# Differential attention's queries and keys projected with a head's columns as rows, the rotary step by rows with a row-swapped load, in place of transposes

## The chip, the cores and the metric

The kernel runs on one core of one Trainium2 chip. The core has TensorE (PE, matrix products; its weight loads are shown as PEld), VectorE (DVE), ScalarE (ACT), GpSimd (POOL), SyncE (SP) and 16 DMA engines. The metric is the device time of one launch in microseconds (us): the median of several runs. Beside it there is one execution recorded by the hardware profiler, from which all durations below come.

## The reference, cut to what matters

Two layers of a hybrid backbone work on 640 tokens of 1024 channels: 128 context tokens, and 512 latent tokens, which also read 128 cached context tokens. Each layer projects the normalised tokens and runs three mixers (retention, differential attention, latent attention), merges them by gates, and ends in a SwiGLU block. The change concerns differential attention with 4 heads, each with two halves of 64 columns for queries and keys:

```python
dq = dq.reshape(B, S, H_DIFF, 2, DIFF_HD)          # h @ w_in, columns of 4 heads x 2 x 64
dk = dk.reshape(B, S, H_DIFF, 2, DIFF_HD)
if rope is not None:                               # latent tokens alone
    dq, dk = _rope(dq, c64, s64), _rope(dk, c64, s64)
dk_all = jnp.concatenate([ck.reshape(B, L, H_DIFF, 2, DIFF_HD), dk], axis=1)

def _rope(x, c, s):                                # c, s of a token's row and column
    x1, x2 = jnp.split(x, 2, axis=-1)              # 32 and 32 columns
    return jnp.concatenate([x1 * c - x2 * s, x2 * c + x1 * s], axis=-1)

def _diff_attention(q, k, v, lam, lam_init):
    s = jnp.einsum('bqhcd,bkhcd->bhcqk', q, k) * DIFF_HD ** -0.5
    p = jax.nn.softmax(s, axis=-1)
    a = p[:, :, 0] - lam * p[:, :, 1]
    o = jnp.einsum('bhqk,bkhe->bqhe', a, v)
    return _head_rmsnorm(o) * (1.0 - lam_init)
```

The context tokens' keys and values are outputs too (`ndk`, `ndv`).

## The kernel before, in words

All numbers are 32-bit. A matrix product is made of three products of operands split in two (`mm3`, lines 131 to 133: high x high, high x low, low x high). `split_hi` (ACT, line 112) rounds a tile to the matmul's format, and `split_lo` (DVE, line 115) takes the rest. `load_w` loads one weight tile of 128 x 1024 on SyncE's queue and splits it.

The stages of a layer follow one another: latent attention (`mla`), its branch projection (`branch_first`), differential attention (`diff`), retention (`ret`), the gates and branches, the output projection and the FFN. Into a stage that waits for softmax, units of projection work are put as filler. `plan(points, (generator, n, t0, t1))` spreads n units over a stage's points; `fill()` at each point issues the units that are due, `flush()` the rest. A planner of the framework then orders the instructions of each engine's queue by a simulated time line; every queue is in order.

`diff_proj` is the filler of latent attention: 30 units on 37 points. For each of two pairs of heads (`hp`) and each of keys, queries and values (`kind` 1, 0, 2) it loads two weight tiles, and for each of five blocks of 128 tokens makes 24 matmuls (8 row blocks of the weights by 3 products) of 256 columns: the tokens are the output's rows (`a_gemm`, activations as the loaded operand, weights streaming). ACT copies a result from the PSUM tile `G` into `stg` (line 791), and GpSimd's queue stores it to DRAM in `dproj` (line 792).

`diff` builds each head's operands in `build(hd)`, which stands one head ahead of `diff_head`. It loads values `V`, keys `rk` (`dproj` and the cache `cdk`, 6 blocks of 128 tokens as rows) and queries `rq` on GpSimd's queue. `rope_in_place` (lines 431 to 442, DVE) rotates four blocks in four instructions. For each two blocks of keys ACT makes the high part `kh`, written twice (line 742), and DVE the low part `kl`; TensorE transposes four high tiles (line 747) and two low tiles (line 748) against `identr` into the PSUM tiles `Tp`; ACT clears the first into `K1` (line 750) and DVE the second into `K2z` (lines 751 and 752). Queries go the same way: `qs` (line 762), two transposes for each block (line 767), and the copy into `Q` (line 769). `K1` holds a half's high part twice, over 128 rows; `Q` holds a half's high and low part one above the other; `K2z` holds a half's low part over zeros. With these, two matmuls make the three products (`diff_head`, lines 825 and 826). Tiles `ra` (`rk`, `rq`), `V`, `K1`, `Q` and `K2z` have two buffers each.

In `diff`, 16 units of gates (line 1013) and 20 of retention's values (lines 805 to 809, stored by GpSimd's queue into `rproj`) are the filler, on 23 points, of which `diff` has 20. `ret` loads `rproj` again.

Of the kernel before, what the change touches and what calls it, by code (L numbers as in the profile page):

```python
# [12 lines left out]
F32 = mybir.dt.float32  # L13
# [34 lines left out]
class Kern:  # L48
# [107 lines left out]
    def setup(self):  # L156
# [7 lines left out]
        self.identr = self.const.tile([P, 128], F32R, name="identr")  # L164
        self.dve.tensor_copy(self.identr, self.ident)
# [264 lines left out]

    def rope_in_place(self, pool, x, b, nb, nh, hd, tag):

        cc, ss = (C_C64, C_S64) if hd == 64 else (C_C32, C_S32)
        hh = hd // 2
        c = self.ct[:, cc + hd * b:cc + hd * (b + nb)].rearrange("p (a d) -> p a d", a=nb).unsqueeze(2).to_broadcast([P, nb, nh, hd])
        s = self.ct[:, ss + hd * b:ss + hd * (b + nb)].rearrange("p (a d) -> p a d", a=nb).unsqueeze(2)
        u = pool.tile([P, nb * nh * hd], F32, tag=tag, name="rp", bufs=1).rearrange("p (a h d) -> p a h d", a=nb, h=nh)
        d = self.dve
        d.tensor_tensor(u[:, :, :, 0:hh], x[:, :, :, hh:hd], s[:, :, :, 0:hh].to_broadcast([P, nb, nh, hh]), op=ALU.mult)
        d.tensor_tensor(u[:, :, :, hh:hd], x[:, :, :, 0:hh], s[:, :, :, hh:hd].to_broadcast([P, nb, nh, hh]), op=ALU.mult)  # L440
        d.tensor_tensor(x, x, c, op=ALU.mult)
        d.tensor_tensor(x, x, u, op=ALU.add)
# [252 lines left out]
    def diff(self, l, act, yhi, ylo, ctx):  # L695
# [20 lines left out]
        a6 = "p (a c r) -> p a c r"  # L716

        def build(hd):
            hp, h = divmod(hd, 2)
            hs = slice(128 * h, 128 * h + 128)  # L720
            V[hd] = pool.tile([P, 6, 128], F32, tag="V", name="V", bufs=2)
# [5 lines left out]

            k1 = K1[hd] = pool.tile([P, 2, TK], F32R, tag="K1", name="K1", bufs=2)
            k2 = K2[hd] = k2z[hd % 2]
            r = pool.tile([P, 6, 128], F32, tag="ra", name="rk", bufs=2)  # L730
            nc.gpsimd.dma_start(out=r[:, 0, :], in_=self.dproj[hp, 1][:, 0, hs])
            nc.gpsimd.dma_start(out=r[:, 1, :], in_=io["cdk"][l, :, 128 * hd:128 * hd + 128])
            nc.gpsimd.dma_start(out=r[:, 2:6, :], in_=self.dproj[hp, 1][:, 1:5, hs])
            nc.gpsimd.dma_start(out=io["ndk"][l, :, 128 * hd:128 * hd + 128], in_=r[:, 0, :])
            rv = r.rearrange("p a (c d) -> p a c d", c=2)
            self.rope_in_place(pool, rv[:, 2:6], 0, 4, 2, 64, "rp")
            for j in range(3):
                x = rv[:, 2 * j:2 * j + 2]
                kh = pool.tile([P, 2, 2, 2, 64], F32R, tag="kh", name="kh", bufs=2)
                kl = pool.tile([P, 2, 2, 64], F32R, tag="kl", name="kl", bufs=2)  # L740
                for i in range(2):
                    a.copy(kh[:, i], x[:, i].unsqueeze(2).to_broadcast([P, 2, 2, 64]))
                self.split_lo(kl, x, kh[:, :, :, 0, :])
                t, t2 = self.Tp(F32R), self.Tp(F32R)
                for i in range(2):
                    for c in range(2):
                        self.pe.transpose(t[:, 256 * c + 128 * i:256 * c + 128 * i + 128], kh[:, i, c].rearrange("p a r -> p (a r)"), self.identr)
                    self.pe.transpose(t2[:, 128 * i:128 * i + 128], kl[:, i].rearrange("p a r -> p (a r)"), self.identr)
                cs = slice(256 * j, 256 * j + 256)
                a.copy(k1[:, :, cs], t.rearrange("p (c n) -> p c n", c=2))  # L750
                d.tensor_copy(k2[0:64, 0, cs], t2[0:64, 0:256])
                d.tensor_copy(k2[64:128, 1, cs], t2[64:128, 0:256])

            q = Q[hd] = pool.tile([P, 2, T], F32R, tag="Q", name="Q", bufs=2)
            r = pool.tile([P, 6, 128], F32, tag="ra", name="rq", bufs=2)
            nc.gpsimd.dma_start(out=r[:, 0:5, :], in_=self.dproj[hp, 0][:, :, hs])
            rv = r.rearrange("p a (c d) -> p a c d", c=2)
            self.rope_in_place(pool, rv[:, 1:5], 0, 4, 2, 64, "rp")
            for b0, nb in ((0, 1), (1, 2), (3, 2)):
                x = rv[:, b0:b0 + nb]  # L760
                qs = pool.tile([P, 2, 4, 64], F32R, tag="kh", name="qs", bufs=2)
                a.copy(qs[:, 0:nb, 0:4:3, :], x)
                self.split_lo(qs[:, 0:nb, 1:3, :], x, qs[:, 0:nb, 0:4:3, :])
                t = self.Tp(F32R)
                for i in range(nb):
                    for c in range(2):
                        self.pe.transpose(t[:, 256 * c + 128 * i:256 * c + 128 * i + 128],
                                          qs[:, i, 2 * c:2 * c + 2, :].rearrange("p a r -> p (a r)"), self.identr)
                a.copy(q[:, :, 128 * b0:128 * (b0 + nb)], t.rearrange("p (c n) -> p c n", c=2)[:, :, 0:128 * nb])
# [643 lines left out]
```

## Time and profile before

| | |
|---|---|
| median of 3 runs | 2487.21 us (2484.67 to 2488.88) |
| profiled execution | 2487.65 us, of which the span from first to last instruction 2485.8 |
| PE, PEld | 2419.1 and 2367.1 us busy, 17236 instructions each |
| DVE, ACT, POOL | 1511.3, 992.8 and 177.0 us busy |
| HBM read, written | 225.97 and 20.22 MB, 99 GB/s over the span |

A row of the profile names the line, engine and operation, then what it writes and reads by the program's names (`Tp<-identr,kh`). A busy time is the union of an engine's instructions; matmuls overlap, so that the spacing of their starts, not their duration, is what each takes of the engine. Where a row has a bracket, the engine was idle that long before it, and the arrow names what ended the wait.

### The profile page before, as it was taken

The numbers are of one execution on the slowest core, as the hardware profiler recorded it, in microseconds if no ns is written. First come the engines' busy times: TensorE is split into PE (matmuls) and PEld (weight loads), VectorE is DVE, ScalarE is ACT, GpSimd is POOL, SyncE is SP. The second block draws the span as 40 slices with busy tenths as digits, with TensorE's granted clock in tenths as the row PEclk, the third lists the DMA queues.
The fourth block names the chain that finished last, engine by engine and source line by source line (L and its number), as shares of the span: only waits on it lengthen the run. The fifth ranks groups of instructions, "written<-read, shape, count | busy, mean of one in ns | idle before, by whom it ended". The sixth has DMA issues, their size and how long they took to land.

```text
span 2485.8 us, 42801 instructions
## 1 busy us (share of the span) xinstructions
PE 2419.1 (97%) x17236; PEld 2367.1 (95%) x17236; DVE 1511.3 (61%) x3463; ACT 992.8 (40%) x2102; POOL 177.0 (7%) x306
## 2 busy tenths in 40 slices
PE   8999999999999999999999999998999999999998
PEld 5999999999999999999999999998999999999997
DVE  5877686566787676485477867764663553333324
ACT  5656565422335221212375655653222352122123
POOL 0000210100010010010000012111000000000001
PEclk9999999999999999999999999999999999999999
DMA  6212322322553454463231123213232222222221
GB/s 263 75 60 63 105 78 65 96 91 70 196 175 111 153 178 153 128 193 102 66 126 55 60 75 114 69 61 126 62 109 69 77 68 85 78 69 76 69 75 62
DMA packets 70677, 248.94 MB, mean 100 GB/s; under 512 B 9840, under 2 KB 10064, under 8 KB 69584
## 3 DMA queue, kind: packets, MB, share of 16 engines
q1 hardware_dynamic: 46944, 164.12, 20.3%
q0 software_dynamic: 23248, 81.36, 10.1%
q8 instruction: 135, 2.21, 0.4%
q10 hardware_dynamic: 288, 0.73, 0.1%
q14 instruction: 62, 0.51, 0.1%
HBM read 225.97 MB, written 20.22 MB: 99 GB/s over the span
## 4 chain that ended last, share of the span: by engine, by line
PE 91%; DVE 4%; issue 2%; ACT 2%; DMA 1%; POOL 0%; DVEq 0%; ACTq 0%; POOLq 0%
PE G L131 13%; PE G L132 12%; PE G L133 12%; PE S L1107 8%; PE S L1106 8%; PE S L1105 8%; PE S L131 6%; PE S L132 6%; PE S L133 6%; PE O L855 1%; PE Tp L658 1%; PE S L825 1%; PE O L633 1%; PE O L632 1%; PE S L826 1%
## 5 line engine op out<-in xcount | busy, mean ns | idle before, releaser
L112 ACT CAST whi<-raw 128x1024 fp32r<-128x1024 f32 (+4 forms) x298 | 299.2, 1018 | 756.5 <-PE G L132 262.5
L115 DVE TENSOR_TENSOR wlo<-raw,whi 128x1024 fp32r<-128x1024 f32 (+4 forms) x298 | 349.2, 1182 | 370.7 <-ACT whi L112 368.6
L131 PE MATMUL G<-ghi,whi 128*128 128x256 f32 (+1 forms) x704 | 217.1, 309 | 3.1 <-DVE x L1067 3.1
L133 PE MATMUL G<-ghi,wlo 128*128 128x384 f32 (+1 forms) x704 | 216.4, 308 | 0.0
L132 PE MATMUL G<-glo,whi 128*128 128x384 f32 (+1 forms) x704 | 216.3, 308 | 0.0
L1105 PE MATMUL S<-h1hi,whi 128*128 128x384 f32 x640 | 214.0, 334 | 0.0
L1106 PE MATMUL S<-h1lo,whi 128*128 128x384 f32 x640 | 213.9, 334 | 0.0
L1107 PE MATMUL S<-h1hi,wlo 128*128 128x384 f32 x640 | 213.9, 334 | 0.0
L1107 PE MATMUL S<-h0hi,wlo 128*128 128x256 f32 x704 | 199.2, 283 | 1.1 <-DVE wlo L115 0.9
L1106 PE MATMUL S<-h0lo,whi 128*128 128x256 f32 x704 | 198.8, 283 | 0.0
L1105 PE MATMUL S<-h0hi,whi 128*128 128x256 f32 x704 | 198.1, 282 | 0.0
L238 DVE SCALAR_TENSOR_TENSOR junk<-rawr,csr 128x1024 bf16<-128x1024 f32 x160 | 195.0, 1219 | 1.3
L131 PE MATMUL G<-whi,h1hi 128*128 128x256 f32 x624 | 179.0, 287 | 1.5 <-DVE mx L449 0.6
L133 PE MATMUL G<-whi,h1lo 128*128 128x256 f32 x624 | 177.2, 284 | 0.0
L132 PE MATMUL G<-wlo,h1hi 128*128 128x256 f32 x624 | 177.2, 284 | 0.0
L1067 DVE SCALAR_TENSOR_TENSOR x<-G,mod,x 128x128 f32<-128x128 f32 (+1 forms) x192 | 77.4, 435 | 138.0 <-PE G L133 137.5
L448 DVE TENSOR_REDUCE mx<-S 128x1 f32<-128x640 f32 (+1 forms) x160 | 113.0, 714 | 49.4 <-PE S L826 28.5
L1107 PEld LDWEIGHTS S<-h0hi,wlo 128*128 128x128 f32 x704 | 134.6, 191 | 2.8 <-DVE wlo L115 2.6
L131 PEld LDWEIGHTS G<-ghi,whi 128*128 128x128 f32 x704 | 132.1, 188 | 4.6 <-DVE x L1067 3.4
L1106 PEld LDWEIGHTS S<-h0lo,whi 128*128 128x128 f32 x704 | 134.3, 191 | 0.3
L1105 PEld LDWEIGHTS S<-h0hi,whi 128*128 128x128 f32 x704 | 134.3, 191 | 0.0
L131 PE MATMUL G<-whi,h0hi 128*128 128x256 f32 x416 | 121.6, 293 | 12.0 <-DVE rvs L808 11.7
(431 smaller groups left out, 6901.8 us busy)
## 6 DMA issues: line engine op xcount, KB each, us to landing
raw<-w_ffn_in SPq DMA_DIRECT2D x88, 512.0 KB, 3.6
rawr<-w_adat POOLq DMA_DIRECT2D x80, 512.0 KB, 4.0
raw<-w_gate SPq DMA_DIRECT2D x48, 512.0 KB, 3.3
raw<-w_ffn_out SPq DMA_DIRECT2D x32, 512.0 KB, 3.7
raw<-w_diff SPq DMA_DIRECT2D x24, 512.0 KB, 3.5
raw<-w_branch SPq DMA_DIRECT2D x24, 512.0 KB, 3.6
raw<-w_ret SPq DMA_DIRECT2D x24, 512.0 KB, 3.5
raw<-w_ada SPq DMA_DIRECT2D x16, 512.0 KB, 9.7
```

Source lines behind the costliest of these rows:

```text
L112: (eng or self.act).copy(hi, src)
L115: (eng or self.dve).tensor_tensor(lo, src, hi.bitcast(F32), op=ALU.subtract)
L131: self.pe.matmul(out, lh, rh, start=i == 0, stop=False)
L132: self.pe.matmul(out, lh, rl, start=False, stop=False)
L133: self.pe.matmul(out, ll, rh, start=False, stop=i == n - 1)
L238: self.tc.keep_in_program_order(d.scalar_tensor_tensor(junk, raw, 1.0, self.csr[:, i, :], op0=ALU.mult, op1=ALU.mult, accum_out=mod[:, n, ...
L448: self.dve.tensor_reduce(mx, sv, axis=AX.XY if len(sv.shape) == 3 else AX.X, op=ALU.max)
L632: self.pe.matmul(o[:, :n], vv, hi, start=i == 0, stop=False)
L1067: self.dve.scalar_tensor_tensor(x[h][:, n, c0:c1], ps[:, c0:c1], g[:, n, gi:gi + 1], x[h][:, n, c0:c1], op0=ALU.mult, op1=ALU.add)
L1105: self.pe.matmul(o, lh, rh, start=k == 0, stop=False)
L1106: self.pe.matmul(o, lh, rl, start=False, stop=False)
L1107: self.pe.matmul(o, ll, rh, start=False, stop=k == nk - 1)
```

## The change

Keys and queries are projected head by head with the weights as the loaded operand and the tokens streaming, so that `dproj` for them is a tile of 128 rows (a head's columns) by 640 tokens: 16 units over halves of 256 and 384 tokens, and 10 units of values in the old form, 26 in the plan. `build` loads a head's rows, and for the rotary step a second copy `u` in which blocks of 32 rows are swapped in pairs, by four loads; three DVE instructions then rotate 512 tokens with tables of cosine and sine by rows, loaded once a stage. ACT and DVE write `K1`, `K2z` and `Q` straight from the rows. The key cache comes in and the new keys go out with columns as rows (the host turns them round). The value loads stand behind those of keys and queries.

```diff
-        self.identr = self.const.tile([P, 128], F32R, name="identr")
-        self.dve.tensor_copy(self.identr, self.ident)
...
+        cosT = self.load_small(pool, [P, 512], io["ropeT"][0], "cosT")
+        sinT = self.load_small(pool, [P, 512], io["ropeT"][1], "sinT")
+        def rotate(src, x):
+            u = pool.tile([P, 512], F32, tag="rs", name="rs", bufs=2)
+            for q in range(4):
+                nc.gpsimd.dma_start(out=u[32 * q:32 * q + 32, :], in_=src[32 * (q ^ 1):32 * (q ^ 1) + 32, 128:640])
+            d.tensor_tensor(x, x, cosT, op=ALU.mult)
+            d.tensor_tensor(u, u, sinT, op=ALU.mult)
+            d.tensor_tensor(x, x, u, op=ALU.add)
         def build(hd):
+            top, low = slice(0, 64), slice(64, 128)
+            src = self.dproj[hd, 1]
+            r = pool.tile([P, TK], F32, tag="ra", name="rk", bufs=2)
+            nc.gpsimd.dma_start(out=r[:, 0:128], in_=src[:, 0:128])
+            nc.gpsimd.dma_start(out=r[:, 128:256], in_=io["cdkT"][l, hd])
+            nc.gpsimd.dma_start(out=r[:, 256:TK], in_=src[:, 128:T])
+            nc.gpsimd.dma_start(out=io["ndk"][l, hd], in_=r[:, 0:128])
+            rotate(src, r[:, 256:TK])
+            for c, own, other in ((0, top, low), (1, low, top)):
+                a.copy(k1[own, c, :], r[own, :])
+                a.copy(k1[other, c, :], r[own, :])
+                self.split_lo(k2[own, c, :], r[own, :], k1[own, c, :])
+            src = self.dproj[hd, 0]
+            r = pool.tile([P, TK], F32, tag="ra", name="rq", bufs=2)
+            nc.gpsimd.dma_start(out=r[:, 0:T], in_=src)
+            rotate(src, r[:, 128:T])
+            for c, own, other in ((0, top, low), (1, low, top)):
+                a.copy(q[own, c, :], r[own, 0:T])
+                self.split_lo(q[other, c, :], r[own, 0:T], q[own, c, :])
             V[hd] = pool.tile([P, 6, 128], F32, tag="V", name="V", bufs=2)
...
-            self.rope_in_place(pool, rv[:, 2:6], 0, 4, 2, 64, "rp")
-            for j in range(3):
...
-            self.rope_in_place(pool, rv[:, 1:5], 0, 4, 2, 64, "rp")
-            for b0, nb in ((0, 1), (1, 2), (3, 2)):
...
     def diff_proj(self, l, act, pool):
...
-            for kind in (1, 0, 2):
-                units = self.load_a(self.io["w_diff"][l, hp, kind], 2, 4, 256)
...
+            for hd in (2 * hp, 2 * hp + 1):
+                for kind in (1, 0):
+                    u = self.load_w(self.io["w_dqk"][l, kind, hd], 1024)
+                    for h in (0, 1):
+                        o, w = HALF[h]
+                        ps = self.G()
+                        self.mm3(ps[:, :w], self.b_steps(*u, 0, KT, act, h))
+                        r = pool.tile([P, 384], F32, tag="stg", name="stg", bufs=2)
+                        self.act.copy(r[:, :w], ps[:, :w])
+                        self.pool.dma_start(out=self.dproj[hd, kind][:, o:o + w], in_=r[:, :w])
+                        yield 1
+            units = self.load_a(self.io["w_dv"][l, hp], 2, 4, 256)
...
-                self.plan(37, (self.diff_proj(l, act, pool), 30, 0.0, 1.0))
+                self.plan(37, (self.diff_proj(l, act, pool), 26, 0.0, 1.0))
```

## Rows read from the trace of the kernel before

**Rows 1.** The page: span, busy time by engine with its share and instructions.

```profile
span 2485.8 us, 42801 instructions
PE 2419.1 (97%) x17236; PEld 2367.1 (95%) x17236; DVE 1511.3 (61%) x3463; ACT 992.8 (40%) x2102; POOL 177.0 (7%) x306
```

**Rows 2.** Busy time by stretch: start:end, length, engines, PE's clock, DMA, GB/s.

```profile
85.00:281.00 196.00, 191.94 (x1498) 186.91 (x1498) 147.34 (x347) 117.63 (x274) 20.42 (x37) 1.00 0.21 68
306.00:493.00 187.00, 180.08 (x1386) 175.57 (x1385) 131.00 (x376) 108.34 (x291) 26.35 (x44) 1.00 0.24 77
...
1529.00:1714.00 185.00, 178.01 (x1369) 173.48 (x1368) 128.32 (x370) 107.20 (x287) 24.72 (x41) 1.00 0.24 77
```

**Rows 3.** PE in order of time (start, duration, what), old projection, 99.8 to 101.9 us.

```profile
99.80 0.28 PE L131 MATMUL G<-whi,h1hi 128*128 128x256 f32 x1
...
101.83 0.28 PE L133 MATMUL G<-whi,h1lo 128*128 128x256 f32 x1
```

**Rows 4.** PE in order of time, a gate unit, 329.6 to 331.8 us.

```profile
329.67 0.33 PE L131 MATMUL G<-h1hi,whi 128*128 128x384 f32 x1
...
331.75 0.33 PE L131 MATMUL G<-h1hi,whi 128*128 128x384 f32 x1
```

**Rows 5.** The transposing lines: instructions, duration ns min/median/max, first and last start.

```profile
L747 PE MATMUL Tp<-identr,kh x96: 222/246/306, 298.4 to 1636.3; 128*128 128x128 f32 x96
...
L748 PE MATMUL Tp<-identr,kl x48: 223/228/281, 302.3 to 1637.1; 128*128 128x128 f32 x48
...
L767 PE MATMUL Tp<-identr,qs x80: 222/244/283, 312.7 to 1642.4; 128*128 128x128 f32 x80
```

**Rows 6.** PE in order of time, a run of six transposes, 305.9 to 306.8 us.

```profile
305.90 0.28 PE L133 MATMUL G<-yhi,wlo 128*128 128x256 f32 x1
306.01 0.46 PE L747 MATMUL Tp<-identr,kh 128*128 128x128 f32 x4
306.31 0.33 PE L748 MATMUL Tp<-identr,kl 128*128 128x128 f32 x2
306.47 0.41 PE L131 MATMUL G<-yhi,whi 128*128 128x384 f32 x1
306.72 0.34 PE L132 MATMUL G<-ylo,whi 128*128 128x384 f32 x1
```

**Rows 7.** PE in order of time, a run of two, 331.9 to 332.5 us.

```profile
331.92 0.34 PE L132 MATMUL G<-h1lo,whi 128*128 128x384 f32 x1
332.10 0.29 PE L767 MATMUL Tp<-identr,qs 128*128 128x128 f32 x2
332.22 0.41 PE L133 MATMUL G<-h1hi,wlo 128*128 128x384 f32 x1
332.47 0.34 PE L131 MATMUL G<-h1hi,whi 128*128 128x384 f32 x1
```

**Rows 8.** PE in order of time, the longest waits ahead of transposes, layer 0.

```profile
327.90 0.36 PE L748 MATMUL Tp<-identr,kl 128*128 128x128 f32 x2 [0.37 <-ACT K L750]
...
362.21 0.34 PE L748 MATMUL Tp<-identr,kl 128*128 128x128 f32 x2 [0.46 <-DVE K2z L752]
```

**Rows 9.** The page's groups: xcount | busy us, mean ns | idle before, releaser.

```profile
L112 ACT CAST whi<-raw 128x1024 fp32r<-128x1024 f32 (+4 forms) x298 | 299.2, 1018 | 756.5 <-PE G L132 262.5
L115 DVE TENSOR_TENSOR wlo<-raw,whi 128x1024 fp32r<-128x1024 f32 (+4 forms) x298 | 349.2, 1182 | 370.7 <-ACT whi L112 368.6
```

**Rows 10.** GpSimd in order of time, DMA issues of the builds, 305 to 362 us.

```profile
306.48 0.75 POOL L733 DMA_DIRECT2D rk<-dproj  x1
...
361.76 0.56 POOL L722 DMA_DIRECT2D V<-cdv  x1 [26.30 <-PE Tp L747]
```

**Rows 11.** DMA issues by tile: xcount, KB each, median us from issue to landing.

```profile
rk<-dproj POOLq DMA_DIRECT2D x8, 256.0 KB, 3.8
...
rk<-dproj POOLq DMA_DIRECT2D x8, 64.0 KB, 2.3
```

**Rows 12.** PE in order of time, its longest wait inside latent attention's heads, layer 0.

```profile
193.22 0.38 PE L632 MATMUL O<-pth,vhl 128*128 128x256 f32 x1 [0.88 <-ACT pth L112]
```

More of the change, by code (lines that the diff above doesn't have):

```diff
@@ L734, in build @@
-            nc.gpsimd.dma_start(out=io["ndk"][l, :, 128 * hd:128 * hd + 128], in_=r[:, 0, :])
-            rv = r.rearrange("p a (c d) -> p a c d", c=2)
-            self.rope_in_place(pool, rv[:, 2:6], 0, 4, 2, 64, "rp")
-            for j in range(3):
[L738 to L757, printed above, removed]
-            self.rope_in_place(pool, rv[:, 1:5], 0, 4, 2, 64, "rp")
-            for b0, nb in ((0, 1), (1, 2), (3, 2)):
[L760 to L769, printed above, removed]
@@ L780, in diff_proj @@
         self.dproj = {}
+        for hd in range(4):
+            for kind in (1, 0):
+                self.dproj[hd, kind] = self.dr.tile([P, T], F32, tag=f"dp{hd}{kind}", name="dproj", bufs=1)
         for hp in range(2):
-            for kind in (1, 0, 2):
-                self.dproj[hp, kind] = self.dr.tile([P, NB, 256], F32, tag=f"dp{hp}{kind}", name="dproj", bufs=1)
+            self.dproj[hp, 2] = self.dr.tile([P, NB, 256], F32, tag=f"dv{hp}", name="dproj", bufs=1)
         for hp in range(2):
-            for kind in (1, 0, 2):
-                units = self.load_a(self.io["w_diff"][l, hp, kind], 2, 4, 256)
-                for b in range(NB):
-                    ps = self.G()
-                    self.a_gemm(ps[:, :256], act, b, units)
-                    r = pool.tile([P, 256], F32, tag="stg", name="stg", bufs=2)
-                    self.act.copy(r, ps[:, :256])
-                    self.pool.dma_start(out=self.dproj[hp, kind][:, b, :], in_=r)
-                    yield 1
+            for hd in (2 * hp, 2 * hp + 1):
+                for kind in (1, 0):
+                    u = self.load_w(self.io["w_dqk"][l, kind, hd], 1024)
[8 more added lines that the diff above has]
+            units = self.load_a(self.io["w_dv"][l, hp], 2, 4, 256)
+            for b in range(NB):
+                ps = self.G()
+                self.a_gemm(ps[:, :256], act, b, units)
+                r = pool.tile([P, 384], F32, tag="stg", name="stg", bufs=2)
+                self.act.copy(r[:, :256], ps[:, :256])
+                self.pool.dma_start(out=self.dproj[hp, 2][:, b, :], in_=r[:, :256])
+                yield 1
     def ret_values(self, l, act, pool):
@@ L1320, in consts, with rope_rows @@
     return c
+def rope_rows(ct):
+    rows = [ct[:, o:o + 256].reshape(128, 4, 64).transpose(2, 1, 0).reshape(64, 512) for o in (C_C64, C_S64)]
+    return np.ascontiguousarray(np.stack([np.concatenate([r, r], axis=0) for r in rows]))
 def ntiles(w):
@@ L1365, in layout @@
     out["w_mla1"] = c(np.stack([pieces(w_mla[l][:, NA:], 4) for l in L]))
-    out["w_diff"] = c(np.stack([[[pieces(wi[l][:, o[4 + j] + 256 * hp:o[4 + j] + 256 * hp + 256], 4) for j in range(3)] for hp in range(2)] for l in L]))
+    out["w_dqk"] = c(np.stack([[ntiles(wi[l][:, o[4 + j]:o[5 + j]]) for j in range(2)] for l in L]))
+    out["w_dv"] = c(np.stack([[pieces(wi[l][:, o[6] + 256 * hp:o[6] + 256 * hp + 256], 4) for hp in range(2)] for l in L]))
     out["w_ret"] = c(np.stack([[pieces(wi[l][:, 256 * j:256 * j + 256], 4) for j in range(6)] for l in L]))
@@ L1403, in unpack @@
     return (c(yt[None, :128]), c(yt[None, 128:]), c(nret[0][None]), c(nret[1][None]),
-            c(r["ndk"].reshape(1, DEPTH, 128, 4, 128)), c(r["ndv"].reshape(1, DEPTH, 128, 4, 128)),
+            c(r["ndk"].transpose(0, 3, 1, 2)[None]), c(r["ndv"].reshape(1, DEPTH, 128, 4, 128)),
             c(r["nckv"][None]), c(r["nkpe"][None]))
```

26 lines of the change are left out of this document (6 added, 20 removed).

## The prediction

> **What bounds the kernel now.** I read the page first, then the busy time by stage, then the order of TensorE's instructions, and last the queues that feed the changed code.
>
> On the page the matmul engine PE is busy for 2419.1 of 2485.8 us, VectorE (DVE) for 61% and ScalarE (ACT) for 40% [rows 1]. A busy PE need not be one at its peak, so the question is whether PE also sets the pace in the two stages that the change touches. The busy times by stretch say so: in 85 to 281 us (latent attention, with the differential projections as filler) PE is busy 191.94 of 196, in 306 to 493 us (differential attention) 180.08 of 187, both at a granted clock of 1.00, that is 2.4 GHz; DVE has 147.34 and 131.00 there. Layer 1 repeats it: 178.01 of 185 in 1529 to 1714 us [rows 2]. So a column that PE no longer streams is time, as long as DVE, ACT and the DMA queues go on delivering.
>
> **Projection of keys and queries.** Before, a projection of one pair of heads is 5 token blocks of 24 matmuls with 256 columns: for 2 pairs and 2 kinds 480 matmuls a layer. After, it is 8 weight tiles, each over 256 and 384 tokens in 24 matmuls: 192 of 256 columns and 192 of 384. The columns are the same, 122,880. What one matmul costs is its spacing from the next: 17 spacings of the old projection take 101.83 - 99.80 = 2.03 us, 0.1194 each [rows 3]; 12 spacings of the gates, whose form the new one takes, 331.75 - 329.67 = 2.08 us for 384 columns, 0.1733 each [rows 4]. Before: 480 x 0.1194 = 57.3 us; after: 192 x 0.1194 + 192 x 0.1733 = 56.2. Gain 1.1 us a layer, 2.2 in all; since starts are rounded to 10 ns, between 1.5 and 3. The values keep their form, and as many weight tiles of the same size are loaded and split as before.
>
> **Transposes.** They go: 96 + 48 for keys and 80 for queries [rows 5], 224 in all. Their durations (228 to 246 ns) are pipelined and are not what they cost. For that I take the matmuls around a run of them: from the start at 305.90 to the start at 306.72 are 0.82 us, in which stand one matmul of 256 columns (0.119), six transposes and one of 384 (0.173): 0.528 us, 0.088 each [rows 6]. A run of two: 331.92 to 332.47 are 0.55, less two of 0.173, 0.204, 0.102 each [rows 7]. Most runs are of two or four, so I take 0.092 between the two: 224 x 0.092 = 20.6 us. The lower end is the spacing inside a run: four between 306.01 and 306.31, 0.075 each [rows 6], so 16.8 us; the upper is 0.102, so 22.8.
>
> Here a rule can be weighed. The Trainium skill, "TensorE: Matmul & The Clock Gate", section "Back-to-back issue gap", gives a single warm matmul as N/2.4 + 2.5 ns, which for 128 columns is 56 ns, and 81 ns where each has its own weight load. By the first the transposes would give back 12.5 us and by the second 18.1; the trace, with 88 and 102 ns, disagrees with the first and lies above the second.
>
> **Waits that the transposes cause.** They wait for PSUM: 0.37 us for ACT to clear a key tile and 0.46 for DVE [rows 8], both on PE itself, and the same again in layer 1: 2 x 0.83 = 1.7 us that go. What was late next in those places is the gate filler, which is ready; bounds 0 and 1.7.
>
> **DVE and ACT.** Per head 20 DVE instructions become 10 (six rotary steps of 512 columns, four splits of 768 or 640), and 15 ACT copies become 6 of 768 or 640 columns on 64 rows. None is longer than the 1024-column forms, 1.18 us on DVE and 1.02 on ACT [rows 9], so at most 11.8 and 6.1 us a head, four heads in 187 us. Neither engine bounds the stage, so I count no gain; the lighter queues could let scores or gate results leave sooner. PE idles 6.9 us in the stage and 7.0 in layer 1 [rows 2]; at best half of that, 7 us, comes back.
>
> **GpSimd's queue and the row-swapped load.** A build had 9 DMAs and has 17: two rotations of four quarter loads each. An issue holds this queue 0.56 us for 64 KB and 0.75 for 256 KB [rows 10]; 8 more are 4.5 us a build, on an engine that is busy 26 of 187 us [rows 2]. I cost them at nothing, because a build is issued one head ahead. The whole of it end to end: 17 x 0.56 = 9.5, two landings of 3.8 [rows 11], 11.8 of DVE and 6.1 of ACT: 35.0 us, against 187/4 = 46.8 us for one head. The cover is 11.8 us. The first build has no head ahead of it, but branch_first and the gates lie there for PE. The value loads move behind keys and queries in the same in-order queue, so that a wait for a free V buffer (26.30 us in the row [rows 10]) now holds the next build instead of its own. The tables of cosine and sine are two loads of 256 KB a layer, 1.5 us of the queue, hidden in the same way. DVE gets one new wait, of the product with the sine table for the four quarter loads; behind it in DVE's order stand the maxima and scalings of the head under way, and ACT's exponentials and PE's next scores wait for those.
>
> One rule speaks against the change: the Trainium skill, "DMA: Bandwidth & Descriptors", section "Rules for kernel authors", says that two transfers to disjoint partition halves serialize. No row shows quarter loads; if the four landed one after the other at the 2.3 us of a 64 KB load [rows 11], a rotation would take 9.2 instead of 3.8, a build 45.8 instead of 35.0, and the cover would shrink from 11.8 to 1.0 us. I take the 3.8: the 256 KB load of the row spans all partitions and moves the same bytes.
>
> **Coarser filler.** The planner puts 26 units instead of 30 on the 37 points of latent attention, so 11 points have none instead of 7; never two in a row, since the step is 1.42. PE idles 4 us in the 196 now. The longest wait on PE in that stage is 0.88 us, for ACT's copy of a transposed probability [rows 12]. Four more empty points a layer cost between 0 and 8 x 0.88 = 7 us; I take 1, by the 4 us that seven empty points and both ends of the stage share now. The coarser unit is 24 x 0.173 = 4.2 us instead of 2.9; one G bank holds it for one ACT copy, as before.
>
> **The sum.** 2.2 + 20.6 + 1.7 - 1.0 = 23.5 us off the profiled execution. That took 2487.65 us, with 1.85 outside the span; it lies 0.4 above the median of 2487.21. So 2487.65 - 23.5 = 2464.2, and the difference to the median is small beside the range: 2464.
>
> **Rivals.**
> - *Only the spacing is saved.* The weight load of a transpose hides behind its neighbours and PE, once free, waits in their place for a softmax or a gate. The transposes give 16.8, the waits nothing, the projections 2.2 and the filler costs 1 to 5: 2487.65 - 16.8 - 2.2 + 1 to 5 = 2470 to 2474. For it: PE has idle gaps with ACT and DVE as releasers. Against: both runs in the rows cost more than that. Chance 0.20, up to 2482. The Trainium skill's spacing of a single matmul ("TensorE: Matmul & The Clock Gate", "Back-to-back issue gap") would give 2487.65 - 12.5 - 2.2 = 2473, in the same place.
> - *More goes.* With DVE and ACT lighter, half of the idle 14 us of differential attention goes too: 2464 - 7 = 2457. For it: two engines lose work that stands in the way of softmax and gates. Chance 0.14.
> - *No change.* The transposes were filler in empty time, and latent attention pays for its coarser units: if each of the 22 empty points of both layers waits the 0.88 us, 19.4 us go, 2464 + 19.4 = 2483. Against: 14 such points cost less than 10 us in all now. Chance 0.10.
> - *Slower.* GpSimd's queue stands for the V buffer, the next build starts late, and PE meets a head whose keys aren't there. It shows from 11.8 us of delay and decides the sign from 11.8 + 23/6 = 15.6; at the 26.30 us of the row, 14.5 are exposed at each of heads 1 to 3 in both layers: 2464 + 6 x 14.5 = 2551. Against: the buffer frees when the head before last is done, and the gates go on meanwhile. Chance 0.08. If quarter loads serialize, as the Trainium skill has it ("DMA: Bandwidth & Descriptors", "Rules for kernel authors"), it would show from 1.0 us of delay.
>
> **How the numbers follow.** The forecast has 0.48 (2459 to 2469). A measurement of this kernel can tell about 0.2%, 5 us, from no change. Faster by more: 0.48 + 0.14 + 0.20 = 0.82; within it 0.10; slower 0.08. The range has to leave out no more than 0.2: above, slower and no change (0.18) lie outside it, below a little of the large gain (0.02). With the bounds of the terms, 2.2 + 22.8 + 1.7 + 7 = 33.7 off gives 2454; 2.2 + 16.8 - 7 = 12.0 off gives 2476, and I go on to 2479, as the scheduler orders the engines anew.
>
> **What would show it.** PE's instruction count falls by 224 + 192 = 416 to 16820. From the end of latent attention to the end of differential attention it is some 11 us less in each layer; latent attention itself is 1 us shorter to 3 longer. The 384-column matmuls of the projection keep 0.173. No wait of PE above 1 us stands ahead of the scores of heads 1 to 3, and the idle time of PE in the two stages stays near 7 and 4 us. The forecast is wrong if PE's idle time in either stage grows by more than 5 us, if PE waits for DVE or ACT where those had waited for a quarter load, or if the spacing of the remaining matmuls changes.

## The result: 0.6% slower, and the profile after

| | before | after |
|---|---|---|
| median | 2487.05 us (2484.67 to 2488.88, 4 runs) | 2502.75 us (2500.34 to 2503.31, 4 runs) |
| after / before, 95% interval | | 1.0062 [1.0044, 1.0079] |
| span of the profiled execution | 2485.8 us | 2500.6 us |

The forecast was 2464 us. The page of the kernel after: span, busy time by engine, and the shares of the chain that ended last.

```profile
span 2500.6 us, 41892 instructions
PE 2413.9 (97%) x16820; PEld 2358.7 (94%) x16820; DVE 1501.7 (60%) x3382; ACT 985.3 (39%) x2022; POOL 202.7 (8%) x366
...
PE 87%; DVE 5%; ACT 4%; issue 2%; DMA 1%; POOL 0%; DVEq 0%; ACTq 0%; POOLq 0%
```

The 416 instructions of PE are gone, PE is 5.2 us less busy than in [rows 1], and DVE and ACT are less busy too; yet the span is 14.8 us longer. A page can't say why. The loss is found by comparing stretches between two events that both kernels have: from branch_first's first matmul to retention's first score, in layer 0 and layer 1, the whole of differential attention. Before:

```profile
281.70:549.30 267.60, 256.05 (x1962) 250.30 (x1962) 177.51 (x491) 135.30 (x341) 36.62 (x60) 0.99 0.27 88
1501.60:1771.00 269.40, 257.44 (x1962) 251.71 (x1962) 177.36 (x491) 135.49 (x341) 36.57 (x60) 0.99 0.27 87
```

After (start:end, length, then PE, PEld, DVE, ACT and POOL busy with instructions, PE's clock, DMA share, GB/s):

```profile
285.10:559.80 274.70, 254.04 (x1850) 247.53 (x1850) 172.18 (x451) 132.03 (x305) 48.53 (x88) 0.96 0.29 92
1513.90:1785.60 271.70, 252.97 (x1848) 246.50 (x1848) 172.23 (x451) 131.91 (x305) 48.34 (x88) 0.97 0.29 93
```

Two things grew: PE's idle time (length less PE's busy time) and the time at a lower clock, 0.96 and 0.97 of full speed instead of 0.99. The stretches at half clock in layer 0 of after, each of which stands as one block in the clock's record (the last is as long as two, and is counted as two below):

```profile
285.10:288.40 3.30, 3.29 (x12) 2.94 (x13) 3.09 (x5) 1.93 (x4) 0.93 (x2) 0.50 0.24 60
343.20:346.50 3.30, 3.30 (x17) 3.30 (x16) 3.08 (x8) 1.36 (x4) 1.63 (x4) 0.50 0.73 233
363.60:366.90 3.30, 3.30 (x15) 3.30 (x15) 2.28 (x9) 2.01 (x8) 1.07 (x2) 0.50 0.66 169
397.80:401.10 3.30, 3.11 (x12) 3.11 (x13) 2.36 (x6) 3.23 (x11) 0.00 (x0) 0.50 0.00 0
510.40:517.10 6.70, 5.62 (x26) 5.63 (x27) 0.80 (x2) 0.86 (x3) 1.94 (x3) 0.50 0.47 165
```

Before has one such block in layer 0, at the border to retention:

```profile
502.20:505.60 3.40, 3.40 (x17) 3.40 (x17) 0.12 (x1) 0.00 (x0) 1.07 (x2) 0.50 0.56 202
```

I count half of the time at half clock as lost. That is the most it can be: the spacings shown below, 0.27 us at half clock and 0.15 at full, make it 0.44. That splits each stage into idle time, clock loss and the rest, which I call work (us; length less idle less half of the time at half clock; all taken unrounded, so that a last digit can differ from the lines above):

| stretch | length | idle | at half clock | work |
|---|---|---|---|---|
| before, layer 0 / 1 | 267.6 / 269.4 | 11.5 / 12.0 | 3.4 / 6.8 | 254.4 / 254.0 |
| after, layer 0 / 1 | 274.6 / 271.7 | 20.6 / 18.7 | 20.4 / 17.0 | 243.8 / 244.5 |
| after less before | +7.0 / +2.3 | +9.1 / +6.8 | +17.0 / +10.2 | -10.6 / -9.5 |

So the transposes' time did go, 10.6 and 9.5 us against a forecast of 10.3 a layer. It was eaten twice: by 15.9 us of new idle time on PE in both layers together, and by up to (17.0 + 10.2)/2 = 13.6 us of lower clock. Latent attention adds the rest: branch_first starts 3.4 us later in layer 0, and takes 1.9 us longer to reach in layer 1. The sum is 7.0 + 2.3 + 3.4 + 1.9 = 14.6 of the 14.8 us.

**Where PE waits.** PE's waits during the four heads of layer 0, by what they waited for (us in total, times, longest). Before, 316.1 to 467 us:

```profile
PE G L131 <- ACT gt L1013: 1.5, 4, 0.6
PE S L825 <- ACT dp L450: 1.0, 2, 0.7
```

After, 318.6 to 472.8 us:

```profile
PE S L816 <- ACT dp L435: 6.2, 4, 3.4
PE G L131 <- ACT gt L1004: 6.0, 5, 3.8
```

`gt` is ACT's copy of a gate out of the one PSUM tile `G`, and `dp` the exponential of a head's scores. Both wait in ACT's queue. In layer 1 the sums are the same, some 2.5 us before and 12.2 after, so these waits grew by over 19 us in all; the other waits of the two stretches shrank. PE in order of time around the first of the long waits:

```profile
337.76 0.42 PE L133 MATMUL G<-h1hi,wlo 128*128 128x384 f32 x1
341.99 0.39 PE L131 MATMUL G<-h0hi,whi 128*128 128x256 f32 x1 [3.82 <-ACT gt L1004]
```

and ACT at the same time:

```profile
335.21 1.05 ACT L112 CAST whi<-raw 128x1024 fp32r<-128x1024 f32 x1 [2.14 <-PE G L132]
336.29 0.84 ACT L730 CAST K<-rk 64x768 fp32r<-64x768 f32 x1
337.15 0.83 ACT L731 CAST K<-rk 64x768 fp32r<-64x768 f32 x1
337.99 0.83 ACT L730 CAST K<-rk 64x768 fp32r<-64x768 f32 x1
338.85 0.83 ACT L731 CAST K<-rk 64x768 fp32r<-64x768 f32 x1
339.70 0.37 ACT L847 ACTIVATE osb<-O,dz 128x128 f32<-128x128 f32 x1
339.97 1.46 ACT L740 CAST Q<-rq 64x640 fp32r<-64x640 f32 x2
341.45 0.49 ACT L1004 ACTIVATE gt<-G 128x384 f32<-128x384 f32 x1
341.96 0.80 ACT L435 ACTIVATE dp<-S,mx 128x640 f32<-128x640 f32 x1
```

The gate unit's last matmul ends at 338.18. Its copy could have run then; it runs at 341.45. In the queue it stands behind the six copies of the next head's build, 4 x 0.83 + 1.46 = 4.8 us (4.9 from start to end where nothing stands between), with one short `osb` between them; at 338.18 some 3 us of that are still to come. These copies are for the next head, whose first score comes at about 356 us; nobody is waiting for them yet. All six became ready at once. For this head it is because keys and queries are rotated over all their columns, and DVE ends both rotations within one microsecond:

```profile
335.57 0.69 DVE L713 TENSOR_TENSOR rk<-rk,rs 128x512 f32<-128x512 f32 x1
336.17 0.69 DVE L713 TENSOR_TENSOR rq<-rq,rs 128x512 f32<-128x512 f32 x1
```

For heads 2 and 3 it is something else. Their rotations end at 352.2 and 372.8 us, but their copies start only at 357.00 and 392.58, 0.6 to 1.0 us after the end of the last score matmuls of heads 0 and 1 (355.98 and 392.01). `K1` and `Q` have two buffers each, so a build can't write them before the head two places ahead has made its scores; then all six copies may go. Where ACT is free at that moment, the trace shows the wait: in the run with the second key copies on DVE, below, the first copy of head 2 starts at 350.56 us, after 0.79 us of waiting for a score matmul.

Before, the same work was cut up by the transposes: a copy waited for its PSUM tile, and others went ahead meanwhile (ACT, 323 to 328 us):

```profile
323.40 0.48 ACT L1013 ACTIVATE gt<-G 128x384 f32<-128x384 f32 x1
323.77 0.58 ACT L750 CAST K<-Tp 128x512 fp32r<-128x512 f32 x1
324.24 0.31 ACT L762 CAST qs<-rq 128x128 fp32r<-128x128 f32 x1
327.26 0.59 ACT L750 CAST K<-Tp 128x512 fp32r<-128x512 f32 x1 [2.71 <-PE Tp L747]
```

The other two builds have the same form, with an exponential behind the six copies instead of a gate: PE waits 2.12 us at 362.41, inside head 1, and 3.40 us at 397.99, at head 2's first scores. ACT ahead of the latter, where the key copies begin at 392.58:

```profile
395.99 1.47 ACT L740 CAST Q<-rq 64x640 fp32r<-64x640 f32 x2
397.48 0.37 ACT L435 ACTIVATE dp<-S,mx 128x128 f32<-128x128 f32 x1
```

With each of the three waits comes a block at half clock (343.2, 363.6 and 397.8 us above). The first two begin some 1.2 us after PE has gone on, the third 0.2 us before. PE at the third:

```profile
397.99 0.63 PE L816 MATMUL S<-K,Q 128*128 128x320 f32 x1 [3.40 <-ACT dp L435]
398.42 0.47 PE L817 MATMUL S<-K2z,Q 128*128 128x320 f32 x1
398.69 0.47 PE L816 MATMUL S<-K,Q 128*128 128x320 f32 x1
```

There the spacing of these matmuls is 0.27 us; after the wait at 362.41, which the clock follows only at 363.6, it is 0.15:

```profile
362.41 0.41 PE L816 MATMUL S<-K,Q 128*128 128x320 f32 x1 [2.12 <-ACT dp L435]
362.66 0.31 PE L817 MATMUL S<-K2z,Q 128*128 128x320 f32 x1
362.81 0.31 PE L816 MATMUL S<-K,Q 128*128 128x320 f32 x1
```

### The profile page after: what moved, and what is told of

Its sections match the earlier page's. It is cut to its first block, busy times and chain, and to the rows that moved or that the text cites. A ratio compares the mean times of both kernels' runs of the same rounds, so it can differ in the third digit from the quotient of the medians.

```text
span 2500.6 us, 41892 instructions
## 1 busy us (share of the span) xinstructions
PE 2413.9 (97%) x16820; PEld 2358.7 (94%) x16820; DVE 1501.7 (60%) x3382; ACT 985.3 (39%) x2022; POOL 202.7 (8%) x366
## 4 chain that ended last, share of the span: by engine, by line
PE 87%; DVE 5%; ACT 4%; issue 2%; DMA 1%; POOL 0%; DVEq 0%; ACTq 0%; POOLq 0%
PE G L131 12%; PE G L132 12%; PE G L133 12%; PE S L1098 8%; PE S L1097 8%; PE S L1096 8%; PE S L131 6%; PE S L132 5%; PE S L133 5%; PE O L846 1%; PE Tp L643 1%; DVE wlo L115 1%; ACT whi L112 1%; PE O L618 1%; PE S L816 1%
## 5 line engine op out<-in xcount | busy, mean ns | idle before, releaser
L132 PEld LDWEIGHTS G<-glo,whi 128*128 128x128 f32 x704 | 132.1, 188 | 0.2
L133 PEld LDWEIGHTS G<-ghi,wlo 128*128 128x128 f32 x704 | 132.2, 188 | 0.0
L131 PE MATMUL G<-whi,h1hi 128*128 128x256 f32 x432 | 124.7, 289 | 0.8 <-ACT rvs L796 0.6
L133 PE MATMUL G<-whi,h1lo 128*128 128x256 f32 x432 | 123.3, 285 | 0.0
```

The costliest lines, as they stand in the source:

```text
L131: self.pe.matmul(out, lh, rh, start=i == 0, stop=False)
L132: self.pe.matmul(out, lh, rl, start=False, stop=False)
L133: self.pe.matmul(out, ll, rh, start=False, stop=i == n - 1)
```

## The theories

- *A, the burst.* A build's six ACT copies stand in one piece of 4.9 us in ACT's in-order queue, ahead of the gate copy and the exponentials that release PE; PE waits, and its clock falls after each wait. Cutting the piece gives the transposes' time back; lengthening it costs more.
- *B, the loads.* The 17 DMAs of a build on GpSimd's queue, or the row-swapped loads, make operands late.
- *C, the projection.* The new projection or its coarser units lose the time in latent attention and after it.

## The experiments

**One part alone.** The first keeps the builds of before and takes the new projection (`diff_proj` of the diff, 26 units); the second takes the new build on the old projection's layout:

```diff
+            src = self.dproj[hp, 1][:, :, hs]
+            nc.gpsimd.dma_start(out=r[:, 256:TK].rearrange("p (a c) -> p a c", a=4), in_=src[:, 1:5, :])
```

> New projection and its 26 filler units, old builds with transposes (they read a head's column rows as if they were token rows, so the scores are not the reference's). Theory A, ACT's burst: six long copies of a build, all ready at once, stand ahead of the gate copies and exponentials in ACT's queue, and PE waits for those; here there is no burst, so differential attention takes what it took before and only latent attention changes: 2483 to 2492 us. Rival C, the coarser filler makes the loss: 2498 to 2506.

Measured: 2489.57 us, 1.0011 [1.0002, 1.0021].

> Old projection with 30 units, new builds by rows (token rows read as column rows, so the scores are not the reference's; the loads have 512-byte runs in place of 2 KB). Theory A: the waits of 2 to 4 us behind the burst and the clock's fall after each stay, 2494 to 2502 us. Rival C: the saved transposes show and nothing else, 2464 to 2470.

Measured: 2480.0 us, 0.9975 [0.9964, 0.9986].

C falls as the main cause: the projection alone costs 2.4 us. But the build alone gained 7 us, which A had not expected. That lies between the expectation of A and that of C. Each part's difference to before is +2.4 and -7.2; together they make +15.7, so some 20 us hang on how the two meet. ACT's order shows what differs: with the old projection a gate copy slips in between the key copies (3.4 us) and the query copies (1.5), and PE's waits for `gt` and `dp` in the heads of layer 0 add up to 5.5 us, the longest 1.5, against 12.2 and 3.8 after.

**Fewer and plainer loads.** The four quarter loads of a rotation become one load of the same bytes without the swap; the rotation then gives another result:

```diff
-            for q in range(4):
-                nc.gpsimd.dma_start(out=u[32 * q:32 * q + 32, :], in_=src[32 * (q ^ 1):32 * (q ^ 1) + 32, 128:640])
+            nc.gpsimd.dma_start(out=u, in_=src[:, 128:640])
```

> The changed kernel, but the second copy of a head is loaded by one DMA without swapping its row blocks (the rotation is then not the reference's): 11 DMAs a build in place of 17. Theory A: same as the changed kernel within 4 us, 2499 to 2507. Rival B, the queue of GpSimd and the quarter loads make the operands late: 2465 to 2485.

Measured: 2495.54 us, 1.0038 [1.0025, 1.0051]. That lies between the expectations. 6 of 17 DMAs less give 7 us back, so B isn't the loss, but neither did the time stay. Some bursts changed: the longest pieces on ACT for the four builds of layer 0 are 4.9, 3.4, 4.9 and 2.5 us. PE's waits for `gt` and `dp` in the heads are 11.4 us in layer 0, the longest 4.6, but only 6.4 in layer 1, against 12.2 in each layer after. Whether the seven microseconds are the loads or the changed bursts, this run doesn't tell.

**The copies written out in steps** between the row blocks of the head under way, so that the program's order has no burst:

```diff
+            ahead = build(hd + 1) if hd < 3 else iter(())
+            next(ahead, None)
+            self.diff_head(pool, Q[hd], K1[hd], K2[hd], V[hd], nlam, lam_init, yhi[:, hd, :], ylo[:, hd, :], ahead)
```

> The changed kernel with the same instructions, but the builds of heads 1 to 3 are issued in steps: loads and rotations before the head ahead of it, then one half of keys or queries (at most two copies) after each of its query blocks. Theory A: no burst of more than 1.7 us on ACT, waits and falls of the clock go, 2464 to 2478. Rival B: as the changed kernel or worse, 2500 to 2510. Rival D, the transposes were filler in time that PE must wait anyway: 2487 to 2500.

Measured: 2500.49 us, 1.0062 [1.0047, 1.0077]. It didn't test what it was meant to: the framework's planner put the copies side by side again, as ACT's row order shows:

```profile
335.62 0.83 ACT L736 CAST K<-rk 64x768 fp32r<-64x768 f32 x1
...
339.29 1.46 ACT L742 CAST Q<-rq 64x640 fp32r<-64x640 f32 x2
340.77 0.49 ACT L1011 ACTIVATE gt<-G 128x384 f32<-128x384 f32 x1
```

The next holds each copy at its place in the program's order:

```diff
-                a.copy(k1[other, c, :], r[own, :])
+                pin(a.copy(k1[other, c, :], r[own, :]))
+                yield
```

> As the build in steps, but for heads 1 to 3 each of ACT's copies is also pinned in ACT's queue behind what was written ahead of it, so that the planner cannot gather them: one or two copies after each query block. Theory A, the burst: no more than 1.7 us of copies in one piece, PE's waits of 2 to 4 us and the falls of its clock behind them go, 2470 to 2484 us (latent attention keeps what it lost). Rivals B and D: no burst was the cause, 2496 to 2506.

Measured: 2493.32 us, 1.0023 [1.0014, 1.0032], 9 us below after, between the two ranges expected. Pieces of up to 4.1 us remained in layer 0, and 9.8 us of PE's waits for `gt` and `dp`. With the pinning and units of the projection cut in two (42 instead of 26), to see whether their size is what latent attention loses by:

> As the run with the copies pinned, and each projection unit of keys and queries is issued in two halves of 12 matmuls (42 units on the 37 points). If the grain of the filler costs latent attention its 2 us a layer, 3 to 5 us below the run with the copies pinned; if the planner mends the grain anyway, the same within 2 us.

Measured: 2492.97 us, 1.002 [1.001, 1.0029], the same as without. Finer units mend nothing.

**The copies on another engine.** All six on GpSimd:

> The changed kernel with the six copies of a build made by GpSimd in place of ACT. Theory A: ACT has no burst, 2470 to 2486 us. Rival B, operands that come late: later still, as GpSimd's queue also issues the loads, 2503 to 2525. Rival D: as the changed kernel, 2498 to 2506.

Measured: 2502.56 us, 1.0059 [1.0044, 1.0074]. A's expectation is missed by 17 us. Two effects mix here: ACT is free, but the same copy takes longer on GpSimd, and the first head's keys come late: from branch_first's first matmul to the first score are 52.8 us instead of 33.7. What A says of the waits did come: those for `gt` and `dp` in the heads of layer 0 fall to 5.9 us, the longest 1.7, and the time at half clock to 20.5. But PE idles as long as after (21.2 and 20.6 us in the two stretches), now in many small waits, and its work there is 2.5 us a layer more, which stays unexplained. So this run shows that taking the burst off ACT isn't enough by itself.

```profile
L730 POOL CAST K<-rk x16: 825/1152/1562, 313.6 to 1650.3; 64x768 fp32r<-64x768 f32 x16
```

Only the two second copies of the keys on DVE:

```diff
-                a.copy(k1[other, c, :], r[own, :])
+                d.tensor_copy(k1[other, c, :], r[own, :])
```

> The changed kernel with the two second key copies of a build made by DVE: four copies of 3.1 us in all on ACT in place of six of 4.9, and 1.7 us more on DVE. Theory A: PE's waits shrink with the burst, by 1 to 2 us each, and some falls of the clock go: 2486 to 2497 us. Rivals B and D: as the changed kernel, 2499 to 2506.

Measured: 2479.91 us (2477.31 to 2482.65), 0.9971 [0.9959, 0.9983]. One line turns the change from 0.6% slower into 0.3% faster, 6 us below the range that A had given. DVE copies in 0.554 us what takes ACT 0.832, and ACT's piece breaks (ACT, 332 to 338 us):

```profile
L731 DVE CAST K<-rk x16: 553/554/557, 312.3 to 1606.4; 64x768 fp32r<-64x768 f32 x16
...
332.86 1.69 ACT L730 CAST K<-rk 64x768 fp32r<-64x768 f32 x2 [1.78 <-DVE rk L713]
334.58 1.05 ACT L112 CAST whi<-raw 128x1024 fp32r<-128x1024 f32 x1
335.53 0.48 ACT L1004 ACTIVATE gt<-G 128x384 f32<-128x384 f32 x1
335.91 1.46 ACT L740 CAST Q<-rq 64x640 fp32r<-64x640 f32 x2
```

The gate copy goes ahead of the query copies, and PE's waits for it shrink from 6.0 us, longest 3.8, to

```profile
PE G L131 <- ACT gt L1004: 3.0, 7, 1.1
...
PE S L816 <- ACT dp L435: 0.9, 2, 0.5
```

In layer 1 the stage then is 269.40 - 258.50 = 10.9 us shorter than before, as forecast, at a clock of 0.99. In layer 0 it is only 3.7 us shorter: PE waits 5.9 us at the border to retention, and 10.2 us are at half clock. Latent attention keeps 4.7 us of loss in both layers. The line for layer 1:

```profile
1502.60:1761.10 258.50, 245.89 (x1848) 240.08 (x1848) 176.74 (x459) 125.47 (x297) 49.26 (x88) 0.99 0.31 98
```

All six copies on DVE, where they can't delay ACT but stand in DVE's own queue:

> The changed kernel with all six copies of a build made by DVE (0.55 us for 768 columns there by the run with the burst of four, against 0.83 on ACT): no burst on ACT, 3.2 us a head more on DVE. Theory A, ACT's burst: at or below the run with the burst of four, 2470 to 2481 us, and no wait of PE over 2 us for a gate or an exponential behind key copies. If what helped there was only a lucky order of the queues: anywhere between 2480 and 2503.

Measured: 2482.54 us, 0.9981 [0.9972, 0.999]. That is 1.5 us above A's range and inside that of the lucky order; but no wait for a gate or an exponential in the heads is longer than 1.7 us, as A had it. Only the query copies on DVE, all four key copies on ACT:

> The changed kernel with the two query copies of a build on DVE: four copies of 3.3 us on ACT, as many as in the run with the burst of four, but other ones. Theory A: as that run, 2476 to 2488 us. If that one was a lucky order: 2490 to 2503.

Measured: 2494.79 us, 1.003 [1.0018, 1.0042], which A's expectation missed. As many copies are on ACT as with the second key copies on DVE, but they stand together, 4 x 0.83 = 3.4 us ahead of a gate copy, and PE waits as long as after:

```profile
PE G L131 <- ACT gt L1004: 7.1, 5, 3.8
```

So A had to be put more narrowly: what counts is what stands ahead of the copy PE waits for when that copy could run, not how many copies ACT has. The length of the piece doesn't settle it either: the build alone has the same pieces (3.4, 3.4 and 2.5 us for heads 1 to 3), but waits of 5.5 us instead of 7.8, the longest 1.5 instead of 3.8. The planner's order decides how much of a piece is still to come when a gate unit ends.

**The burst made longer**, by making the second key copies twice:

```diff
                 a.copy(k1[other, c, :], r[own, :])
+                a.copy(k1[other, c, :], r[own, :])
```

> The changed kernel with the two second key copies made twice: eight copies, 6.6 us in one piece on ACT in place of 4.9, same result. Theory A: each of PE's waits grows by up to 1.7 us, 6 builds ahead and the stretches at half clock behind them: 2508 to 2518 us. Rivals B and D, the burst is not what PE waits for: 2500 to 2506.

Measured: 2507.38 us, 1.0078 [1.0061, 1.0095], between the two ranges expected. The two copies of 0.83 us more a build are 13.3 us of ACT, an engine that is idle 61% of the time, and the kernel loses 4.0 us by them (0.0016 of 2487), beside 4.6 by the medians; the intervals overlap, but each of its four executions took longer than each of after's. It isn't the test of A that it was meant to be. The planner set the added copies apart: in layer 0 the piece grew to 5.8 us for head 1 and stayed at 4.9 for heads 2 and 3. And the three waits didn't grow: 3.85, 1.90 and 2.67 us, where after has 3.82, 2.12 and 3.40. What grew is the time at half clock, a new wait of 1.5 us for the key copies themselves, and the wait at the border to retention (7.1 us in layer 0). Its profiled execution took 2512.32 us, 4.9 more than its median.

**Both repairs together**, old projection and second key copies on DVE:

> The run with the build alone (old projection and filler, token rows read as column rows, so the scores are not the reference's), with the two second key copies on DVE as in the run with the burst of four. If the two causes add, the burst and the filler of latent attention: the run with the burst of four less what the projection alone cost, 2474 to 2479 us. If the new projection costs only through the place of the bursts: 2479 to 2484.

Measured: 2476.91 us, 0.9963 [0.9949, 0.9978]. The difference to the same edit with the new projection is 0.0008 of 2487, 2 us, with intervals that overlap: no more than what the projection costs by itself. The 20 us by which the parts had missed adding up are gone.

**The price of the transposes.** The last run puts 28 transposes a head, as many as before, back beside e7's edit, with results that nobody uses:

```diff
+            for j in range(7):
+                t = self.Tp(F32R)
+                for i in range(4):
+                    x = k1[:, i // 2, 128 * (i % 2 + 2 * (j % 3)):][:, 0:128]
+                    self.pe.transpose(t[:, 128 * i:128 * i + 128], x, self.identr)
```

> The run with the burst of four, with 28 transposes a head of the finished key tile put back on PE, into the two Tp banks, their results unused (224 in all, no copies with them). If the price of 0.092 us is right and the stage runs at PE's pace: 20.6 us above the run with the burst of four, 2498 to 2503. If much of the saved work only comes back as PE's waits for gates and exponentials: 2484 to 2492.

Measured: 2501.85 us, 1.0053 [1.0037, 1.007], against 0.9971 without them: 0.0082 of 2487 are 20.4 us, and the medians differ by 21.9. For 224 transposes that is 0.091 to 0.098 us each.

The runs side by side, all in us. Pieces are the longest runs of copies on ACT for heads 1 to 3 of layer 0, from start to end; waits of PE for `gt` and `dp` are those in the heads of layer 0; half clock is the sum over the two stretches. All but the median are of the one profiled execution.

| kernel | copies that stand together on ACT | PE's waits | half clock | median |
|---|---|---|---|---|
| second key copies on DVE | 1.7, 1.7, 2.4 | 3.9 | 13.6 | 2479.91 |
| build alone | 3.4, 3.4, 2.5 | 5.5 | 17.0 | 2480.0 |
| all on DVE | none | 5.4 | 13.6 | 2482.54 |
| before | up to 2.3 | 2.5 | 10.2 | 2487.05 |
| pinned, half units | 2.5, 1.7, 4.1 | 10.0 | 20.4 | 2492.97 |
| pinned | 2.5, 1.7, 4.1 | 9.8 | 27.3 | 2493.32 |
| query copies on DVE | 3.4, 3.4, 2.5 | 7.8 | 34.2 | 2494.79 |
| one plain load | 3.4, 4.9, 2.5 | 11.4 | 27.3 | 2495.54 |
| in steps | 3.4, 4.9, 4.9 | 12.7 | 30.7 | 2500.49 |
| all on GpSimd | none | 5.9 | 20.5 | 2502.56 |
| after | 3.4, 4.9, 4.9 | 12.2 | 37.4 | 2502.75 |
| key copies doubled | 5.8, 4.9, 4.9 | 12.3 | 54.6 | 2507.38 |

Before stands for itself, since of these it alone streams the transposes; the build alone has the old projection, some 2 us cheaper by the measurement of the projection alone. Where after, and the run in steps, show 3.4 us for head 1, the two query copies follow behind one short `osb`. Among the others the median mostly rises with the time at half clock and with the waits; the copies on GpSimd are the large exception. That is a correlation over edits each of which also changes the planner's order, not a price for either.

## Why the prediction was wrong

**The step that failed** is "DVE and ACT": "Neither engine bounds the stage, so I count no gain". It added up what ACT does in a head, found 6.1 us at most of 46.8, and took that for harmless. The total held (4.8 us of copies a build). But PE didn't wait for ACT's total; it waited for one copy, and that one stood behind whatever was queued ahead of it. The question to ask was how long the longest run of ready instructions becomes when the step that metered them is removed, and who is behind it. The rows for it stood in the trace of before. [rows 8] show only one side, that transposes waited until a key copy had cleared their PSUM tile; the other side is the row of ACT at 327.26 us above, where a key copy waited 2.71 us until transposes had filled one. So the transposes were also a brake which spread ACT's copies. Six copies at 0.8 us, ready together, can hold a gate copy for up to 4.9 us; PE's waits came out at 3.8, 2.1 and 3.4 us, in place of a forecast of none above 1. The part of the prediction on GpSimd's queue even names the danger, exponentials and next scores behind something in an in-order queue, but on DVE and for the quarter loads.

**A second term was missing.** After a wait of PE the sum had it go on at full speed. With each of the three waits came 3.4 us at half clock, up to 1.7 us lost on top of a wait of 2 to 4. Over both layers the clock took up to 13.6 us, nearly as much as the idle time's 15.9. The blocks at the six waits make 10.2 of them; the rest are two blocks of layer 0, one at the start of branch_first and a second at the border to retention, that before doesn't have. That the waits caused the blocks is not shown: other runs have waits as long without one (last section).

**A third term was mis-sized.** The coarser filler was put at +1.0 us within 0 to 7. The projection alone measured +2.4 where its spacing alone would give -2.2, so the filler, with all else that the projection alone changes, costs some 4.6 us: inside its bounds, more than four times the value taken. Its place is known, its mechanism not: PE's waits from 40 to 281 us are several small ones for DVE and ACT, none above 1.0 us, before and after, and cutting the units in two changed nothing. In layer 0 a block at half clock at 278.2 us, which before doesn't have, is up to 1.7 of the 3.4 us.

**What held.**
- The price of a transpose: 0.092 us by [rows 6, 7], 0.091 to 0.098 by the run that puts them back, and 10.6 and 9.5 us a layer by the work in the stretches. Some of that is waits and clock: in the two stretches the profiled run with the transposes back is 12.3 and 13.0 us longer than the one without them, of which 9.6 and 9.0 are work in the sense of the table, 0.086 and 0.080 each. The Trainium skill's "TensorE: Matmul & The Clock Gate", section "Back-to-back issue gap", gives 56 ns for a single warm matmul of 128 columns and 81 ns in a stream where each has its own weight load. The first, which that section says is too low at small sizes, is too low here by every measure; the second agrees with the 80 and 86 ns of work and lies between the 75 inside a run of [rows 6] and the 88 to 102 around whole runs.
- PE's count, 416 less, and the spacing of the projection's matmuls: 22 spacings of 256 columns from 119.83 to 122.46 us are 0.1195 each, as in [rows 3].
- No wait of PE in the heads ends with a quarter load. Eight issues keep GpSimd's queue for 3.94 us, and a load lands 2.1 us (median) after its issue:

```profile
336.54 3.94 POOL L710 DMA_DIRECT2D rs<-dproj  x8 [15.60 <-DVE rk L713]
...
DMA to landing us min/median/max: 2.0/2.1/4.2
```

  The four loads of a rotation are issued 0.5 us apart. The rule that two transfers to disjoint partition halves serialize (the Trainium skill, "DMA: Bandwidth & Descriptors", section "Rules for kernel authors"), weighed in the prediction at 9.2 us a rotation, doesn't show in these landings; loads issued closer together were not tried. The bracket, 15.60 us for a free buffer of `rs`, is a wait of the kind that the rival of the late operands feared. These loads are head 2's, whose copies ended at 361.9, 36 us ahead of its first score; head 1's had waited 16.0 us, and its copies ended at 341.4, some 14 us ahead.

**The rivals.** None of those named is what happened. The one on the slower side put the loss in GpSimd's queue; it lay in ACT's. "No change" put it in latent attention, where 5.3 us are lost against before, 6.5 of the 38 that are missing against the forecast. The prediction's own test, that PE's idle time may not grow by over 5 us in the stage, and that no wait above 1 us stands ahead of the scores of heads 1 to 3, failed on both counts (9.1 and 6.8 us; 3.40 us at 397.99), and it pointed to the right place.

**What stays open.** Why the planner's order for the new projection lets gates and exponentials end up behind the copies and that for the old one doesn't, and how much of each difference between two runs is only another order, since every edit plans all queues anew; whether a third buffer of `K1` and `Q` would spread the copies of heads 2 and 3; what lets the clock fall at some waits and not at others; what the seven microseconds of the plain load are; why latent attention takes 2 to 3 us more; and PE's wait at the border to retention, which differs among all these kernels (4.16 us before, 5.75 after) and carries two of after's blocks at half clock in layer 0.

## What to carry to other kernels

Before a step is removed, ask what it metered: if transposes or PSUM tiles had spread an engine's work, their removal can make all of it ready at once, and an in-order queue may run it as one piece ahead of whatever PE waits for next. Size such an edit by the longest piece on the helper engine against the slack of the copy behind it, not by the engine's busy share; and allow for time at half clock on top of a wait of 2 us or more. Where a burst shows, moving a part of it to the engine that does it faster can be enough, as the one line here that makes 2502.75 into 2479.91 us; but read the new order from the trace, since moving another part of it gave back only 8 us.

## What the runs showed of the hardware

- In after, each of six waits of PE of 2.1 to 3.8 us in the heads came with one block of 3.4 us at a granted clock of 0.50 (1.2 GHz), where the clock otherwise was 1.00. The wait's length alone doesn't decide it. The run with the projection alone waits 3.19 us at the border to retention in layer 0 and has no block in either stretch; the run with the transposes put back has a wait of 2.47 us in layer 0 with a block (364.6 us) and one of 2.48 in layer 1 without (1594.3); waits of 2.11 us (one plain load, 331.3) and 2.32 (pinned, half units, 340.1) have none either, while one of 1.95 (second key copies on DVE, 391.3) has.
- The same copy of 64 x 768 numbers took 0.554 us on DVE, 0.832 on ACT and 1.15 to 1.31 (median) on GpSimd.
- Two of a build's six copies, 0.83 us each on an engine that is busy 39% of the span, made a difference of 22.8 us, with the order of the queues that each placing brought: 2502.75 with them on ACT, 2479.91 with them on DVE.
